# Sample columns of the gate/up projections: from chunk 0 into the combined products, in both FFNs

## The chip, the cores and the metric

The kernel runs on one core of a Trainium2 chip. The metric is the device time of one execution in microseconds; before the change three runs gave 1936.32, 1937.20 and 1937.89 us, so the median is 1937.2 us. All arithmetic is float32. The large matmuls use the type float32r on operands that are split into a high and a low part, so that each product takes three matmuls.

## The reference

One layer of a hybrid decoder trunk is computed for 1024 prompt tokens and for 64 sample tokens (8 sequences of 8), with shared weights and a model width of 1024:

```
x = x + 0.5 * rms_norm(swiglu(rms_norm(x, g1), ffn1_w_gu, ffn1_w_down), p1)
h = rms_norm(x, gm);  z = h @ w_in + b_in
    attention heads: window 128 with sinks; samples against a cache of 128 keys
    recurrent heads: gated linear recurrence in chunks of 64, state 128 x 128 per head
x = x + rms_norm(concat(norm(attention), gate(recurrence)) @ w_out, pm)
x = x + 0.5 * rms_norm(swiglu(rms_norm(x, g2), ffn2_w_gu, ffn2_w_down), p2)

swiglu(x): g, u = split(x @ w_gu);  (silu(g) * u) @ w_down      # w_gu: 1024 x 5632, w_down: 2816 x 1024
```

All rows of `x @ w_gu` are independent of each other, so a token may be computed in any group of columns.

## The kernel before, in words

**Tokens.** Three chunks: chunk 0 holds 256 prompt tokens and the 64 sample tokens (320 columns), chunks 1 and 2 hold 384 prompt tokens each (`WIDTH`, L26). Activations lie with features on partitions and tokens along the free axis.

**Gate and up of chunk 0.** For each of the 22 column tiles `j` of the gate weights and its partner of the up weights, eight row blocks are accumulated with three matmuls each (`mm3`, L260 to L262). `load_w` brings a 128x1024 weight tile into one of three raw buffers, ScalarE casts it to the high part (`wsph`, L240) and VectorE subtracts it to get the low part (`wspl`, L241). The gate then goes through silu and is multiplied with the up part (`gated0`, L712 to L728). In the first FFN the matmuls run before the norm's factor is known, so gate and up are each multiplied with the factor `rb` afterwards.

**Gate and up of chunks 1 and 2.** They are computed together, by seven products in place of eight: the token chunks and the two halves of the features make a 2x2 block matrix, and the feature halves and gate/up of the weights another (`CHAIN`, `factor`, `product`, `evict`, L751 to L815). There are 22 units `u` with 7 products of 4 row blocks. The left operands are the seven factors `SF[1..7]` (sums and differences of the activations, `sums_s`, L525 to L538), each split into high and low parts by `factor` (L466). For the first FFN the stream `p1` makes them while the chunk-0 columns run; for the second FFN the streams `c1` and `c2` do.

**Where chunk 0 runs.** In the first FFN, 18 of 22 columns run ahead of the combined products; the last four run as `piece`s between the products of the first four units, with the weight tiles that these units have split anyway. In the second FFN, the columns are used as work for TensorE beside the mixer: 4 before the end of the second chunk's mixer, 9 and then 1 before the third chunk's output projection, and 8 after it (`HEAD2`, L1681).

**What sets the order.** The program is written as streams (generators), which `tick` advances by a rate for each step of the main work; `need` runs a stream to its end. A scheduler then lays down the order of each engine. An engine works in its order, so a matmul that waits holds all behind it.

**Down projections.** Chunk 0's activations are read back from a DRAM buffer (`acts`) and multiplied with the down weights (320 columns); chunks 1 and 2 use seven products again, in pairs, from the DRAM buffers `FA`, `FB`, `FH`.

## Time and profile before

| | |
|---|---|
| median of three runs | 1937.2 us |
| span of the profiled execution, first to last instruction | 1937.4 us |
| TensorE busy | 1923.1 us (99%) |
| VectorE busy | 1430.7 us (74%) |
| ScalarE busy | 946.0 us (49%) |
| GpSimd busy | 186.1 us (10%) |
| DMA | 375.56 MB, 194 GB/s on the mean |
| mean granted TensorE clock | 0.999 |

The profile gives no time for the profiled execution beside its span; the span lies 0.2 us above the median of the runs. In the rows, PE is TensorE, PEld its weight loads, DVE VectorE, ACT ScalarE, POOL GpSimd, SP the engine that issues most transfers. The length of a matmul in a row includes its passage through the array; how fast matmuls follow each other is read from their starts. Names such as `mm<-h,wsph` stand for output and inputs.

### The profile page before, as it was taken

What the parts mean: (1) busy time and instruction counts of PE and PEld (TensorE: products, weight loads), DVE (VectorE), ACT (ScalarE), POOL (GpSimd) and SP (SyncE); (2) the same over time, 40 slices, a digit from 0 to 9 for tenths busy, and PEclk for the clock granted to TensorE, in tenths of its full rate; (3) what the DMA queues carried; (4) which work ended last, traced back from release to release, by engine and by line L of the source; (5) the groups of instructions that cost most, each with busy time, mean ns of one, the idle gap of its engine ahead of it and who ended that gap; (6) DMA issues with size and microseconds to landing.
All of it is one profiled execution on the core that took longest, in us unless ns stands there. A gap on an engine that the chain in (4) does not pass through costs nothing.

```text
span 1937.4 us, 34843 instructions
## 1 busy us (share of the span) xinstructions
PE 1923.1 (99%) x13547; PEld 1806.1 (93%) x13547; DVE 1430.7 (74%) x2469; ACT 946.0 (49%) x1701; POOL 186.1 (10%) x227
## 2 busy tenths in 40 slices
PE   9999999999999999999999999999999999999998
PEld 9999999999998987788999888989999999999886
DVE  6896789877568666787678758756987887656666
ACT  5553444444455434545445545846544444445452
POOL 0300000000004022020221212000000000000102
PEclk9999999999999999999999999999999999999999
DMA  6643676555767556765334344546555555667974
GB/s 248 209 133 115 232 267 247 206 191 184 242 217 242 180 155 215 283 220 163 114 102 153 99 140 142 164 147 209 185 198 192 198 188 189 210 228 241 308 255 141
DMA packets 175750, 375.56 MB, mean 194 GB/s; under 512 B 16144, under 2 KB 67536, under 8 KB 175568
## 3 DMA queue, kind: packets, MB, share of 16 engines
q1 hardware_dynamic: 169680, 362.84, 56.0%
q10 hardware_dynamic: 5904, 10.49, 1.5%
q8 instruction: 106, 1.74, 0.4%
q14 instruction: 60, 0.49, 0.1%
HBM read 290.86 MB, written 83.39 MB: 193 GB/s over the span
## 4 chain that ended last, share of the span: by engine, by line
PE 88%; DMA 6%; DVE 3%; ACT 1%; issue 1%; POOL 1%; SPq 0%; ACTq 0%; DVEq 0%; POOLq 0%
PE mm L260 27%; PE mm L262 26%; PE mm L261 26%; DMA ar<-fa 1%; DMA xt<-in_x_rest_dram 1%; DMA ar<-act 1%; PE lv L1337 1%; PE sc L1237 1%; DMA raw<-in_ffn_w_gu_dram 1%; PE pv L1283 1%; DVE w L241 1%; PE pT L1269 1%; PE c L262 0%; PE c L260 0%; PE c L261 0%
## 5 line engine op out<-in xcount | busy, mean ns | idle before, releaser
L260 PE MATMUL mm<-h,wsph 128*128 128x320 f32 (+1 forms) x1344 | 427.2, 319 | 0.4 <-DVE big L814 0.4
L261 PE MATMUL mm<-h,wsph 128*128 128x320 f32 (+1 forms) x1344 | 425.5, 317 | 0.2 <-DVE h L241 0.2
L262 PE MATMUL mm<-h,wspl 128*128 128x320 f32 (+1 forms) x1344 | 422.6, 316 | 0.0
L241 DVE TENSOR_TENSOR wspl<-raw,wsph 128x1024 fp32r<-128x1024 f32 x208 | 260.8, 1255 | 125.2 <-ACT wsph L240 124.1
L240 ACT CAST wsph<-raw 128x1024 fp32r<-128x1024 f32 x208 | 217.8, 1049 | 254.0 <-PE mm L261 199.3
L260 PEld LDWEIGHTS mm<-h,wsph 128*128 128x128 f32 x1344 | 252.2, 188 | 4.2 <-issue 2.3
L261 PEld LDWEIGHTS mm<-h,wsph 128*128 128x128 f32 x1344 | 252.5, 188 | 3.9 <-issue 2.3
L262 PEld LDWEIGHTS mm<-h,wspl 128*128 128x128 f32 x1344 | 251.9, 188 | 3.4 <-issue 3.1
L240 ACT CAST w<-raw 128x512 fp32r<-128x512 f32 (+1 forms) x208 | 153.8, 745 | 199.9 <-PE mm L261 96.2
L261 PE MATMUL mm<-h,w 128*128 128x384 f32 (+1 forms) x736 | 245.6, 334 | 0.3 <-DVE h L622 0.3
L260 PE MATMUL mm<-h,w 128*128 128x384 f32 (+1 forms) x736 | 245.7, 334 | 0.2 <-ACT h L620 0.2
L262 PE MATMUL mm<-h,w 128*128 128x384 f32 (+1 forms) x736 | 239.6, 333 | 0.5 <-POOL w L613 0.4
L241 DVE TENSOR_TENSOR w<-raw,w 128x512 fp32r<-128x512 f32 (+1 forms) x208 | 178.3, 861 | 72.6 <-ACT w L240 71.7
L261 PE MATMUL mm<-w,h 128*128 128x512 f32 x462 | 180.5, 391 | 0.7 <-DVE w L241 0.7
L260 PE MATMUL mm<-w,h 128*128 128x512 f32 x462 | 180.8, 394 | 0.0
L262 PE MATMUL mm<-w,h 128*128 128x512 f32 x462 | 179.8, 391 | 0.0
L260 PE MATMUL mm<-big,w 128*128 128x384 f32 x528 | 176.7, 335 | 0.3 <-ACT big L806 0.2
L261 PE MATMUL mm<-big,w 128*128 128x384 f32 x528 | 176.5, 334 | 0.0
L262 PE MATMUL mm<-big,w 128*128 128x384 f32 x528 | 176.0, 334 | 0.0
L261 PEld LDWEIGHTS mm<-h,w 128*128 128x128 f32 x736 | 138.1, 188 | 1.1 <-DVE h L622 0.8
L260 PEld LDWEIGHTS mm<-h,w 128*128 128x128 f32 x736 | 138.1, 188 | 0.8 <-ACT h L620 0.5
L262 PEld LDWEIGHTS mm<-h,w 128*128 128x128 f32 x736 | 137.6, 188 | 1.0 <-POOL w L613 0.7
(367 smaller groups left out, 3353.8 us busy)
## 6 DMA issues: line engine op xcount, KB each, us to landing
raw<-in_ffn_w_gu_dram SPq DMA_DIRECT2D x162, 512.0 KB
raw<-in_ffn_w_down_dram SPq DMA_DIRECT2D x74, 512.0 KB
raw<-in_w_in_dram SPq DMA_DIRECT2D x54, 512.0 KB
ar<-fa SPq DMA_DIRECT2D x70, 384.0 KB
big<-in_ffn_w_down_dram SPq DMA_DIRECT2D x88, 256.0 KB
fb<-big SPq DMA_DIRECT2D x44, 512.0 KB
fa<-big SPq DMA_DIRECT2D x22, 768.0 KB
raw<-fb SPq DMA_DIRECT2D x30, 512.0 KB
```

The lines of the kernel that those rows point to most:

```text
L240: made['S'] = S.copy(hi, src).ins
L241: (lo_eng or V).tensor_tensor(lo, src, hi.bitcast(F32), op=ALU.subtract)
L260: PE.matmul(out, a[0], b[0], start=first, stop=False, skip_group_check=resume)
L261: PE.matmul(out, a[0], b[1], start=False, stop=False, skip_group_check=resume)
L262: return PE.matmul(out, a[1], b[0], start=False, stop=last, skip_group_check=resume).ins
L1237: PE.matmul(banks[g][rows(hq), i, cs], zq[rows(g), 2 * pr + i, b * P + 64 * hq:b * P + 64 * hq + 64], kx[rows(g), k0 + cs.start:k0 + cs.st ...
L1269: PE.transpose(tb2[hq][:, g, i, slot], pt[g][rows(hq), c:c + P], ident[rows(hq), rows(hq)])
L1283: PE.matmul(ob[par][rows(g), :, hq], vn[rows(par), b + (blk + hq) // 2, rows(g)], pT[hq][rows(par), g, :, PLACE[hq][blk]], start=alone or ...
L1337: PE.matmul(b5[32 * i:32 * i + 32, b, a], K[:, a, cs], Q[:, a, cs], start=True, stop=True)
```

## The change

The 64 sample columns leave chunk 0 for the gate and up projections of both FFNs: chunk 0 streams `WU` = 256 columns, and chunks 1 and 2 carry 32 samples each, `WS` = 416 columns. The sample columns of the gated product are stored from the combined units into `acts` (a new small store in each unit), so the down projection stays as it is with 320 columns. In the first FFN the norm's factor is no longer multiplied to the up part; it is kept in DRAM (`rootd`) and multiplied to the chunk-0 prompt columns when the down projection leaves PSUM. In the second FFN the mixer's output stage writes the sample columns to DRAM (`extra`), and the combined operands read them from there.

All 22 columns of chunk 0 now run ahead of the combined products in both FFNs, so the `piece`s and the eighth split weight are gone. The combined products no longer wait for the whole stream of factors in the program: `product` advances the stream until its own factor is there (`feed`). One of the factors' subtractions goes to GpSimd. In the second FFN the columns are spread 3, 8 + 1 and 10 where they were 4, 9 + 1 and 8.

The wider tiles need room. The pools of small buffers shrink (`t2` 8 to 7, `small` 10 to 5, `wf` 4 to 3), and masks and constants of the mixer are made in the mixer or kept in DRAM. The norm's gain of the attention output is applied after the transpose.

```diff
+WU, XT = 256, 32
+WS = 384 + XT
...
-        return pp.tile([P, 4, w], F32R, tag=f"h{w}", bufs=8 if w == 384 else 4, name=uid("h"))
+        return pp.tile([P, 4, WS if w == 384 else w], F32R, tag=f"h{w}", bufs=8 if w == 384 else 4, name=uid("h"))
-    def big(dt=F32, shape=(P, 4, 384)):
+    def big(dt=F32, shape=(P, 4, WS)):
...
+    def feed(name):
+        gen = streams[name][0]
+        while True:
+            yield next(gen)
...
-        return pp.tile([P, 4, 8], F32, tag="small", bufs=10, name=uid("sm"))
+        return pp.tile([P, 4, 8], F32, tag="small", bufs=5, name=uid("sm"))
...
-    def tmp2(name, shape=(P, 512)):
-        return pp.tile(list(shape), F32, tag="t2", bufs=8, name=uid(name))
+    def tmp2(name, shape=(P, 512), dt=F32):
+        return pp.tile(list(shape), dt, tag="t2", bufs=7, name=uid(name))
...
     def factor(SF, m, src):
-        hi, lo = SF[m] = new(), new()
+        hi, lo = new(), new()
         S.copy(hi, src)
         yield
-        V.tensor_tensor(lo, src, hi.bitcast(F32), op=ALU.subtract)
+        (G if m in (5,) else V).tensor_tensor(lo, src, hi.bitcast(F32), op=ALU.subtract)
+        SF[m] = hi, lo
...
         def gated0(j, g, rb):
-            w = WIDTH[0]
+            w = WU
...
             def rest(u):
-                v = u
-                if rb is not None:
-                    v = tmp2("su")
-                    V.tensor_tensor(v[:, :w], u[:, :w], rb, op=ALU.mult)
-                V.tensor_tensor(t[:, :w], t[:, :w], v[:, :w], op=ALU.mult)
-                return nc.sync.dma_start(acts[:, j], t[:, :w]).ins
+                V.tensor_tensor(t[:, :w], t[:, :w], u[:, :w], op=ALU.mult)
+                return nc.sync.dma_start(acts[:, j, :w], t[:, :w]).ins
...
         def product(u, m):
+            while m not in f.SF:
+                next(f.feed)
             c, first, last = CHAIN[m]
             if first:
                 chains[u, c] = mmbank()
-            bk = chains[u, c][:, :384]
+            bk = chains[u, c][:, :WS]
...
             elif m == 3:
                 V.tensor_tensor(e[:, 1], bk, e[:, 1], op=ALU.add)
                 act(0)
+                nc.sync.dma_start(acts[:, j, WU:].rearrange("p (h t) -> p h t", h=2), e[:, 0:3:2, 384:])
...
                         if kp == NK - 1:
-                            S.copy(y[hf][:, i, :w], bank[:, :w])
+                            if tag == 1:
+                                V.tensor_tensor(y[hf][:, i, :WU], bank[:, :WU], rt, op=ALU.mult)
+                                S.copy(y[hf][:, i, WU:w], bank[:, WU:w])
+                            else:
+                                S.copy(y[hf][:, i, :w], bank[:, :w])
...
-            V.scalar_tensor_tensor(o[:r], o[:r], sm[:r, 1, 0:1], aon[:r], op0=ALU.mult, op1=ALU.mult)
+            S.activation(o[:r], o[:r], AF.Copy, scale=sm[:r, 1, 0:1])
...
-    RA0, RA1, RB0, RB1 = 1.2, 0.75, 0.6, 0.8
-    HEAD1, HEAD2 = 9, (4, 13, 22)
+    RA0, RA1, RB0, RB1, RB2 = 1.2, 0.75, 0.6, 0.8, 1.1
+    HEAD1, HEAD2 = NK, (3, 11, 22)
...
+        xs.append(load_x(1))
         for j in first[3:]:
+            if j == first[3]:
+                stream("p1", p1(), P1)
             stored = f1.up0(j, w0)
-            if j in XAT:
+            if j == first[3]:
                 with tc.issue_after(stored):
-                    xs.append(load_x(len(xs)))
...
-        f1.begin(units(HEAD1))
-        need("p1")
+        f1.begin(UNITS)
+        f1.feed = feed("p1")
...
-        f2.begin(units(NK))
-        need("c2")
+        f2.begin(UNITS)
+        f2.feed = feed("c2")
```

How the order moves, at three places.

TensorE, where the first FFN goes from chunk 0 to the combined products. `mm` with 320 columns is chunk 0, `c` a piece of it beside the units; before:

```order
L262 MATMUL mm_1450<-h_143,wspl_1377 128x320
L260 MATMUL mm_1513<-h_142,wsph_1413 128x320
L261 MATMUL mm_1513<-h_144,wsph_1413 128x320
L260 MATMUL c_266_1658<-h_142,w_1576 128x320
L261 MATMUL c_266_1658<-h_144,w_1576 128x320
L262 MATMUL mm_1513<-h_142,wspl_1414 128x320
```

and now:

```order
L245 MATMUL mm_1740<-h_136,wsph_1682 128x256
L246 MATMUL mm_1740<-h_134,wspl_1683 128x256
L244 MATMUL mm_1821<-h_723,w_1800 128x416
L245 MATMUL mm_1821<-h_724,w_1800 128x416
L246 MATMUL mm_1821<-h_723,w_1800 128x416
```

The pieces are gone: 256-column matmuls stand up to the last, and then only 416-column products.

VectorE, in the first FFN's chunk-0 columns, where the sums and factors are made (`wspl`: the low part of a weight tile; `sg`: gate and product; the wide `big`: sums, and `L460` a factor's low part). Now:

```order
L225 TENSOR_TENSOR wspl_1233<-raw_1230,wsph_1232 128x1024
L521 TENSOR_TENSOR big_1170<-big_1169,big_409 128x1664
L523 TENSOR_TENSOR big_494<-big_409,big_494 128x1664
L225 TENSOR_TENSOR wspl_1272<-raw_1269,wsph_1271 128x1024
L186 TENSOR_TENSOR lbe<-cols,lbe 128x4
L187 TENSOR_TENSOR lbe<-cols,lbe 128x4
L710 TENSOR_TENSOR sg_1303<-mm_1267,rb_307 128x256
L714 TENSOR_TENSOR sg_1227<-sg_1227,mm_1191 128x256
L225 TENSOR_TENSOR wspl_1309<-raw_1306,wsph_1308 128x1024
L525 TENSOR_TENSOR big_410<-big_410,big_1170 128x1664
L460 TENSOR_TENSOR h_1301<-big_495,h_1300 128x1664
L460 TENSOR_TENSOR big_1186<-big_1170,big_1185 128x1664
```

The wide rows were 1536 elements long and are 1664 now, and a column has two rows of 256 where it had three of 320.

TensorE, at the last attention block of the third chunk, in the second FFN's chunk-0 columns (`sc`: scores, `pT`: transposes of the probabilities, `pv`: their product with the values). Before, the end of the 33 matmuls between `sc` and `pT`:

```order
L262 MATMUL mm_14023<-h_11489,wspl_13883 128x320
L260 MATMUL mm_14023<-h_11489,wsph_13882 128x320
L261 MATMUL mm_14023<-h_11491,wsph_13882 128x320
L262 MATMUL mm_14023<-h_11489,wspl_13883 128x320
L260 MATMUL mm_14023<-h_11489,wsph_13882 128x320
L1269 MATMUL pT_13953<-ident,t_2011_13924 128x64
```

and now all that stands there:

```order
L1254 MATMUL sc_13911<-kx_10609,big_10724 64x192
L246 MATMUL mm_14051<-hh_11548,wspl_14061 128x256
L244 MATMUL mm_14051<-hh_11548,wsph_14060 128x256
L245 MATMUL mm_14051<-hh_11548,wsph_14060 128x256
L246 MATMUL mm_14051<-hh_11548,wspl_14061 128x256
L1286 MATMUL pT_13949<-ident,t_2000_13920 128x64
```

Four chunk-0 matmuls are left between the scores and the transposes, and after them `pv` follows with no chunk-0 matmul between.

295 lines of the change are left out of this document (156 added, 139 removed).

## The prediction, as put on record

> **What bounds the kernel now.** I read the page's first part, then the share of busy time by stage, then the matmul groups with their shapes kept apart, then single matmuls in order of time. The page's busy row comes first:
>
> ```profile
> PE 1923.1 (99%) x13547; PEld 1806.1 (93%) x13547; DVE 1430.7 (74%) x2469; ACT 946.0 (49%) x1701; POOL 186.1 (10%) x227
> PE 88%; DMA 6%; DVE 3%; ACT 1%; issue 1%; POOL 1%; SPq 0%; ACTq 0%; DVEq 0%; POOLq 0%
> ```
>
> TensorE is busy 99% of the span and carries 88% of the chain that ended last (second row). Busy is not the same as at its peak, so I look at three stages: the first FFN's chunk-0 columns, its combined products, and the second FFN's combined products (columns: stretch, its length, busy us and instructions of PE, PEld, DVE, ACT, POOL, clock, DMA share, GB/s).
>
> ```profile
> 100.00:150.00 50.00, 50.00 (x336) 50.00 (x335) 48.28 (x66) 25.91 (x35) 0.00 (x0) 1.00 0.46 146
> 310.00:360.00 50.00, 50.00 (x290) 50.00 (x289) 44.23 (x79) 23.37 (x46) 0.00 (x0) 1.00 0.65 235
> 1390.00:1500.00 110.00, 110.00 (x636) 110.00 (x636) 92.63 (x160) 48.97 (x96) 0.00 (x0) 1.00 0.56 195
> ```
>
> In order of time (start us, length us), runs of matmuls of 320, of 384 and of 512 columns, first and last of each:
>
> ```profile
> 22.97 0.30 PE L260 MATMUL ax<-h,w 128*128 128x320 f32 x1
> ...
> 29.86 0.31 PE L262 MATMUL ax<-h,w 128*128 128x320 f32 x1
> ...
> 349.83 0.33 PE L262 MATMUL mm<-big,w 128*128 128x384 f32 x1
> ...
> 351.91 0.33 PE L262 MATMUL mm<-h,w 128*128 128x384 f32 x1
> ...
> 1799.81 0.39 PE L260 MATMUL mm<-w,h 128*128 128x512 f32 x1
> ...
> 1803.66 0.39 PE L262 MATMUL mm<-w,h 128*128 128x512 f32 x1
> ```
>
> The ends lie 47, 12 and 17 matmuls apart. That is a start every 0.1466 us at 320 columns, 0.1733 at 384 and 0.2265 at 512. The three lie on one line: 0.41667 ns for each column and 13.3 ns for each matmul (0.1467, 0.1733, 0.2267). 290 matmuls in 50 us and 636 in 110 us are that step and nothing else. So the stages that this change touches most are bound by the number of columns that TensorE streams, and not by a wait.
>
> **What the change removes and adds on TensorE.** It leaves the number of matmuls alone and moves columns. Chunk 0 has 22 column tiles of the gate and 22 of the up weights, 8 row blocks each, 3 matmuls each: 1056 in an FFN, 2112 in both. They go from 320 to 256 columns. The combined products are 22 units x 7 products x 4 blocks x 3 = 1848 in an FFN, 3696 in both (the groups below: 3 x (704 + 528)). They go from 384 to 416.
>
> ```profile
> L260 PE MATMUL mm<-h,w 128*128 128x384 f32 x704 | 235.4, 334 | 0.0
> L260 PE MATMUL mm<-big,w 128*128 128x384 f32 x528 | 176.7, 335 | 0.3 <-ACT big L806 0.2
> L260 PE MATMUL c<-h,w 128*128 128x320 f32 x64 | 19.7, 308 | 0.0
> ```
>
> *Chunk 0.* No float32r matmul of 256 columns is in the trace. The line gives 0.1200 us, so 2112 x 0.0267 = 56.3 us less. The nearest rows bound it: 320 columns from above (0.1467, no gain), and from below the narrowest pairs of a 128-column weight load and a matmul that stand back to back:
>
> ```profile
> 1004.18 1.03 PEld L1461 LDWEIGHTS u<-big,t 128*128 128x128 f32 x8
> ```
> ```profile
> 1004.35 1.05 PE L1461 MATMUL u<-big,t 128*128 128x128 f32 x8
> 1005.24 0.49 PE L1138 MATMUL vT<-ident,t 128*128 128x128 f32 x3
> ```
>
> Eight pairs take 1005.24 - 1004.35 = 0.89 us, 0.111 each (gain at most 2112 x 0.0356 = 75 us). I take the line, since 0.120 lies above the fastest pair seen.
>
> *Combined products.* 416 lies between two measured widths; the line gives 0.1867, so 3696 x 0.0133 = 49.3 us more. If the step stayed at 0.1733 it would be nothing, and at the 512 step 3696 x 0.0534 = 197 us; three points on a line leave little room for either.
>
> TensorE's own account is therefore -56.3 + 49.3 = **-7.0 us**, a small difference of two large terms. Of these, the addition is sure, because the combined stages have no slack. The gain is only real if weights still arrive in time at the faster pace.
>
> The Trainium skill, page "TensorE: Matmul & The Clock Gate", section "Back-to-back issue gap", gives a sustained pace of loads and matmuls of about 81 ns at 128 columns and 131 ns at 512, which is 0.13 ns a column; by it the account would be -17.6 + 15.4 = -2.2 us. This trace does not agree: 0.2267 us at 512 columns, and 0.42 ns a column.
>
> **Whether the narrower stage is fed.** A column tile is 24 matmuls: 3.52 us now, 24 x 0.120 = 2.88 us then. Preparing it costs one load, one cast and one subtraction; the other rows of this stage (window 36 to 165 us) are the products with the factor and the first factors of the combined products:
>
> ```profile
> L241 DVE TENSOR_TENSOR wspl<-raw,wsph 128x1024 fp32r<-128x1024 f32 x26 | 35.0, 1346 | 6.1 <-ACT wsph L240 6.1
> L725 DVE TENSOR_TENSOR su<-mm,rb 128x320 f32<-128x320 f32 x15 | 7.3, 484 | 0.4 <-PE mm L262 0.4
> L471 DVE TENSOR_TENSOR h<-big,h 128x1536 fp32r<-128x1536 f32 x4 | 7.0, 1748 | 0.0
> ```
> ```profile
> L240 ACT CAST wsph<-raw 128x1024 fp32r<-128x1024 f32 x25 | 26.2, 1047 | 26.1 <-PE mm L261 18.2 <-DMA raw<-in_ffn_w_gu_dram 6.1 <-issue 1.1
> ```
>
> ACT mostly waits for TensorE (18.2 of 26.1 us): it runs as far ahead as four pairs of weight tiles allow. The lead is then three tiles less cast and subtraction; at 2.88 us, 8.6 - 1.05 - 1.22 = 6.4 us. What eats it is the end of the factors (sums and first factors) on VectorE. Here is what it eats today, the subtraction of two tiles and TensorE's first matmul with each:
>
> ```profile
> 100.44 1.22 DVE L241 TENSOR_TENSOR wspl<-raw,wsph 128x1024 fp32r<-128x1024 f32 x1
> 122.33 1.22 DVE L241 TENSOR_TENSOR wspl<-raw,wsph 128x1024 fp32r<-128x1024 f32 x1
> ```
> ```profile
> 109.04 0.31 PE L260 MATMUL mm<-h,wsph 128*128 128x320 f32 x1
> ...
> 126.64 0.31 PE L260 MATMUL mm<-h,wsph 128*128 128x320 f32 x1
> ```
>
> The lead falls from 7.4 us (109.04 - 101.66) to 3.1 (126.64 - 123.55) over five tiles, and TensorE does not stall. In the changed order the same stretch has, over six tiles, 8 wide operations (1.67 us from start to start, times 416/384: 1.81), 6 subtractions (1.14) and 7 products of 256 columns (0.34), with 0.5 for small ones: 24.2 us of VectorE for 6 x 2.88 = 17.3 us of TensorE. That eats 6.9 of the 6.4 us: a stall of **+0.5 us**. Ends: 0 if the lead is fuller, 6.9 if there is none. The fifth factor's subtraction, which goes to GpSimd, lengthens neither. The second FFN has more of this work before its last ten columns, so I count nothing there. The product `su` and its copy are dropped: VectorE had cover for them, so they gain nothing.
>
> **Where cover goes in the mixer.** The second FFN's chunk-0 columns also fill TensorE while attention runs. Between the second chunk's last block and the third output projection, 9 columns now stand for 10, and narrower ones: 51.8 us for 70.4. The order shows where it runs out: at the last attention block, 33 matmuls of 0.147 us stood between its scores and the transposes of its probabilities; now 4 of 0.120. The chain that they covered (a score group, the last maximum, the last exponential, the transposes, their copy, the product with the values):
>
> ```profile
> 1265.51 0.83 PE L1237 MATMUL sc<-kx,big 64*64 64x192 f32 x16
> 1266.27 0.41 PE L261 MATMUL mm<-h,wsph 128*128 128x320 f32 x1
> ...
> 1272.22 0.59 PE L1269 MATMUL pT<-ident,t 64*128 64x64 f32 x12
> ...
> 1273.66 0.89 PE L1283 MATMUL pv<-t,vn 64*64 64x128 f32 x24 [0.36 <-DVE t L1274]
> ```
> ```profile
> 1269.59 0.19 ACT L1255 ACTIVATION_READ_ACCUMULATOR t<-t,sm 128x1 f32 x1
> ```
>
> Scores are issued by 1266.27 and the exponentials end at 1269.78: 3.5 us, of which 0.5 is covered now, so 3.0 open. From the transposes' end to the product is 0.85 us (1272.81 to 1273.66), with nothing between in the new order, there and at the block before. Together 4.7, less the 0.36 that is lost there already: 4.3. I take **+3.5**, because at the block before, the transposes stand in two pieces with others between, so their first copy can start early. Ends: 0 (the softmax ends before TensorE gets there) and 4.3.
>
> **Counted at nothing:** the factor's product at the first down projection (on VectorE instead of ScalarE, behind 18 matmuls of the other banks, 18 x 0.147 = 2.6 us; without that cover 0.4 us each for four banks); the strided stores of the left factors and the reload of masks (DMA share 0.46 to 0.65 above); the mixer's constants, moved behind the down products. SP's queue gains 44 small stores of sample columns, each waiting for a product on VectorE with the next raw loads behind it. It waits for VectorE in the combined stage already, without TensorE feeling it (window 310 to 460 us: us, times, longest):
>
> ```profile
> SPq L826 <- DVE big L825: 17.1, 5, 3.5
> ```
>
> If a raw load came late by such a wait in each unit, 22 x 3.5 = 77 us would be the price in one FFN; the loads of a unit are issued a unit (15.7 us) ahead, so I see no path for it.
>
> Sum against the profiled execution's 1937.4: -7.0 + 0.5 + 3.5 = -3.0, 1934.4. The runs' median is 0.2 lower, so **1934.2 us**, 0.16% faster. A change under 0.2% (3.9 us) can't be told from none here, so this sits at the edge of what shows.
>
> **Rivals.**
> *The waits vanish* (the exponentials end early, the lead holds): the full -7.0, 1930.2. For it: a column fewer leaves 2 x (1.05 + 1.22) us less of casts and subtractions beside that chain on ScalarE and VectorE. Against: the adjacent rows in the order.
> *The raw buffers set the pace* (slower). A tile's buffer is used again after three tiles: 8.64 us. A load takes
>
> ```profile
> 299.83 4.31 DMA raw<-in_ffn_w_gu_dram
> ```
>
> plus issue 0.33, cast 1.05 and subtraction 1.22: 6.9 us, so 1.7 us of waiting are free. VectorE is busy 48.28 of 50 us there, so waits of 2 to 3 us are likely at times. If the mean turn is 9.5 us, a tile takes 3.17, and over the 58 tiles that have no mixer beside them 58 x 0.29 = 17 us are lost: about 1951.
> *The weight load sets the pace* (slower). The loads above stand (1.03 - 0.19) / 7 = 0.120 us apart. If the matmul's 13.3 ns come on top, a step is 0.133 and the gain 2112 x 0.0137 = 29 us: 1962. Against: the matmuls of those same loads started 0.111 apart. The same page, section "LDWEIGHTS (loading the stationary operand)", gives 107 ns for 128 columns, under the 0.111 seen, and so speaks against this rival.
> *Fewer small buffers* (`t2` 7 for 8, `small` 5 for 10) make attention and recurrence wait for each other in the mixer, some 6 us: 1940.
>
> **How the numbers follow.** Forecast 0.58 (1930.5 to 1938), waits vanish 0.13, raw buffers 0.13, weight load 0.05, small buffers 0.11. Faster by over 0.2% (below 1933.3): 0.13 and 0.27 of the forecast, 0.40. Slower by over 0.2% (above 1941.1): 0.13 + 0.05 + 0.06 of the small buffers, 0.24. Within: 0.36. The range for 8 in 10 is 1929 to 1943; the slow rivals beyond it hold 0.18.
>
> **What would show it.** Right: starts 0.120 us apart at 256 columns and 0.187 at 416; under 2 us of TensorE idle before the first combined product; a gap of about 3 us between the last block's scores and transposes. Wrong: a step at 256 columns other than 0.120 (0.002 us there is already 4.2 us), ACT waiting for the raw loads and TensorE for `wspl` in the chunk-0 stages, or waits of attention for `sm`.

## The result: slower by 2.2%, and the profile after

The changed kernel takes 1981.04 us (median of 4 runs, 1977.39 to 1983.25) against 1937.55 us before (4 runs, 1936.32 to 1939.19): 1.0219 times as long, 95% interval 1.0204 to 1.0234. The forecast was 1934.2, the range 1929 to 1943. The profiled execution spans 1975.7 us, 38.3 more than before; it is the fastest of the four (1977.39 us, mean granted clock 0.997), and the others took 1980.6 to 1983.3 us at 0.992 to 0.994, so what follows accounts for 38 us and not for the 43.5 between the medians.

The page's first part and its chain, after:

```profile
PE 1945.5 (98%) x13547; PEld 1807.3 (91%) x13547; DVE 1454.2 (74%) x2474; ACT 963.1 (49%) x1719; POOL 202.2 (10%) x230
PE 78%; DMA 8%; DVE 7%; ACT 3%; issue 2%; POOL 1%; SPq 0%; ACTq 0%; DVEq 0%; POOLq 0%
```

TensorE's share of the chain falls from 88% to 78%: waits for VectorE and for transfers have come into it. The same three stretches as in the prediction (stretch, length, busy us and instructions of PE, PEld, DVE, ACT, POOL, clock, DMA share, GB/s):

```profile
100.00:150.00 50.00, 46.57 (x367) 45.57 (x367) 41.17 (x49) 24.78 (x32) 4.73 (x1) 1.00 0.53 175
310.00:360.00 50.00, 50.00 (x266) 49.52 (x265) 43.22 (x74) 22.27 (x42) 0.00 (x0) 1.00 0.59 209
1390.00:1500.00 110.00, 109.02 (x576) 107.43 (x576) 88.06 (x147) 46.22 (x87) 0.00 (x0) 1.00 0.53 183
```

In the chunk-0 stretch TensorE now stands still for 3.4 of 50 us. In the combined stretches it is busy as before (109.02 of 110 us in the second), with fewer instructions. Runs of matmuls of 256, 416 and 512 columns in order of time (start us, length us), first and last of each:

```profile
64.49 0.28 PE L245 MATMUL mm<-h,wsph 128*128 128x256 f32 x1
...
67.13 0.28 PE L246 MATMUL mm<-h,wspl 128*128 128x256 f32 x1
...
349.47 0.35 PE L246 MATMUL mm<-big,w 128*128 128x416 f32 x1
...
351.92 0.35 PE L246 MATMUL mm<-h,w 128*128 128x416 f32 x1
...
1899.23 0.39 PE L244 MATMUL mm<-w,h 128*128 128x512 f32 x1
...
1903.19 0.40 PE L246 MATMUL mm<-w,h 128*128 128x512 f32 x1
```

They lie 22, 13 and 17 matmuls apart: a start every 0.1200, 0.1885 and 0.2329 us. The line of the prediction (0.41667 ns a column and 13.3 ns) gives 0.1200, 0.1867 and 0.2267. The narrow step is exact; 416 columns are 2 ns too long, and the 512-column products, whose width the change does not touch, are 6 ns longer than before. Over all neighbouring matmuls of one width the means are 0.1735 (384) and 0.2274 (512) before, 0.1890 (416) and 0.2332 (512) after.

I cut both traces at the same matmuls, and set each stretch against what its float32r matmuls take on the line (us, before and after):

| from, to | length | change | of it on the line | rest |
|---|---|---|---|---|
| start, first combined product | 136.6, 144.7 | +8.1 | -0.6 | +8.7 |
| first FFN, combined products | 353.5, 355.6 | +2.1 | -2.8 | +4.9 |
| to the mixer's first scores | 231.3, 231.5 | +0.2 | 0.0 | +0.2 |
| to the last block's transposes | 549.6, 539.2 | -10.4 | -22.1 | +11.7 |
| to the second FFN's first combined product | 101.9, 106.2 | +4.3 | -6.1 | +10.4 |
| second FFN, combined products | 325.0, 354.6 | +29.6 | +24.5 | +5.1 |
| to the last matmul | 230.8, 235.4 | +4.6 | +0.2 | +4.4 |

The line sums to -6.9, as forecast (-7.0). What was missed is 45 us in the last column. Some 18 us are the longer steps: 8 at 416 columns and 10 at 512, worked out in the section on the prediction; they are most of the three rows that hold hardly a wait (both combined stages and the last stretch). Of the other 27 us, 16 are idle time of TensorE (span less busy time: 14.3 before, 30.2 after), and up to 5 are two stretches at half clock that follow waits (an estimate: half their length; last section). The rest is not attributed. The longest waits of TensorE in the first head (up to 146 us) and from the mixer to the second FFN (733 to 1379 us), after (us in total, times, longest):

```profile
PE rb L279 <- POOL ss L295: 2.6, 1, 2.6
PE mm L244 <- DVE sg L710: 2.6, 2, 1.4
...
PE mm L244 <- DVE sg L714: 1.0, 1, 1.0
...
PE mm L246 <- DVE wspl L225: 2.7, 2, 2.3
PE pv L1300 <- DVE t L1291: 2.7, 2, 1.8
PE pT L1286 <- ACT t L1272: 1.7, 2, 1.5
PE mm L244 <- ACT sg L1059: 1.5, 2, 0.9
PE mm L244 <- ACT h L1223: 1.1, 1, 1.1
```

Of these only the pair of `pT` and `pv` was foreseen. Is it VectorE's time that holds TensorE in the heads, or do the weights arrive late? ScalarE does wait longer for raw loads: in the first head 26.0 us (9.2 before). But around TensorE's later waits in the first head, and around the long one for `wspl` in the second, VectorE has hardly an idle moment (columns as above; VectorE is the third busy time):

```profile
92.00:118.00 26.00, 22.71 (x184) 21.96 (x183) 26.00 (x25) 15.68 (x15) 6.85 (x1) 1.00 0.41 139
1342.00:1364.00 22.00, 18.62 (x149) 17.81 (x148) 21.89 (x15) 13.27 (x13) 4.84 (x1) 1.00 0.30 107
```

So there it is VectorE's queue that is late, and not a load.

### The profile page after: what moved, and what is told of

The parts are those of the page before. It is cut to its first block, busy times and chain, and to the rows that moved or that the text cites. A ratio compares the mean times of both kernels' runs of the same rounds, so it can differ in the third digit from the quotient of the medians.

```text
span 1975.7 us, 35138 instructions
## 1 busy us (share of the span) xinstructions
PE 1945.5 (98%) x13547; PEld 1807.3 (91%) x13547; DVE 1454.2 (74%) x2474; ACT 963.1 (49%) x1719; POOL 202.2 (10%) x230
## 4 chain that ended last, share of the span: by engine, by line
PE 78%; DMA 8%; DVE 7%; ACT 3%; issue 2%; POOL 1%; SPq 0%; ACTq 0%; DVEq 0%; POOLq 0%
PE mm L244 24%; PE mm L246 24%; PE mm L245 24%; DMA raw<-in_ffn_w_gu_dram 4%; DVE wspl L225 2%; ACT wsph L224 1%; DMA big<-in_ffn_w_down_dram 1%; PE lv L1354 1%; DMA ar<-fa 1%; DMA ar<-act 1%; PE pv L1300 1%; DVE w L225 1%; DVE t L748 1%; PE sc L1254 0%; PE pT L1286 0%
## 5 line engine op out<-in xcount | busy, mean ns | idle before, releaser
L225 DVE TENSOR_TENSOR wspl<-raw,wsph 128x1024 fp32r<-128x1024 f32 x216 | 268.9, 1247 | 120.6 <-ACT wsph L224 113.2
L224 ACT CAST wsph<-raw 128x1024 fp32r<-128x1024 f32 x216 | 226.1, 1048 | 250.5 <-PE mm L245 157.2
L244 PE MATMUL mm<-h,wsph 128*128 128x320 f32 (+2 forms) x1056 | 328.4, 313 | 3.9 <-DVE sg L710 2.6
L245 PE MATMUL mm<-h,wsph 128*128 128x320 f32 (+2 forms) x1056 | 328.6, 311 | 0.1
L246 PE MATMUL mm<-h,wspl 128*128 128x320 f32 (+2 forms) x1056 | 326.8, 310 | 0.8 <-DVE wspl L225 0.6
L246 PE MATMUL mm<-h,w 128*128 128x416 f32 (+1 forms) x736 | 257.1, 350 | 0.7 <-POOL w L607 0.5
L244 PE MATMUL mm<-h,w 128*128 128x416 f32 (+1 forms) x736 | 256.4, 348 | 0.2
L245 PE MATMUL mm<-h,w 128*128 128x416 f32 (+1 forms) x736 | 255.0, 346 | 0.6 <-DVE h L616 0.3
L244 PEld LDWEIGHTS mm<-h,wsph 128*128 128x128 f32 x1056 | 198.8, 189 | 8.6 <-issue 4.1
L245 PEld LDWEIGHTS mm<-h,wsph 128*128 128x128 f32 x1056 | 199.6, 189 | 4.1 <-issue 3.3
L246 PEld LDWEIGHTS mm<-h,wspl 128*128 128x128 f32 x1056 | 199.4, 189 | 2.9 <-DVE wspl L225 1.5
L246 PE MATMUL mm<-big,w 128*128 128x416 f32 x528 | 186.3, 353 | 1.3 <-DVE w L225 1.3
L244 PE MATMUL mm<-big,w 128*128 128x416 f32 x528 | 185.6, 351 | 0.4 <-ACT big L796 0.4
L245 PE MATMUL mm<-big,w 128*128 128x416 f32 x528 | 184.7, 350 | 0.0
L224 ACT CAST w<-t 128x512 fp32r<-128x512 f32 x176 | 108.1, 619 | 94.1 <-PE mm L246 91.3
L245 PEld LDWEIGHTS mm<-h,w 128*128 128x128 f32 x736 | 138.4, 188 | 3.2 <-DVE h L616 1.2
L244 PEld LDWEIGHTS mm<-h,w 128*128 128x128 f32 x736 | 138.2, 188 | 1.9 <-ACT big L798 0.4
```

Source lines behind the costliest of these rows:

```text
L224: made['S'] = S.copy(hi, src).ins
L225: (lo_eng or V).tensor_tensor(lo, src, hi.bitcast(F32), op=ALU.subtract)
L244: PE.matmul(out, a[0], b[0], start=first, stop=False, skip_group_check=resume)
L245: PE.matmul(out, a[0], b[1], start=False, stop=False, skip_group_check=resume)
L246: return PE.matmul(out, a[1], b[0], start=False, stop=last, skip_group_check=resume).ins
```

## The experiments

Three theories were to be told apart from rivals: that the long steps come from where operands lie in SBUF; that chunk-0 tiles had been cover for other engines, so that making them shorter is worth less than the line says; and that the new waits come from single edits (a subtraction on GpSimd, fewer buffers, the mixer's new code). Times are medians, each beside runs of the kernel before on the same chip (1936.9 to 1938.4 in every comparison).

**The first term alone.** The kernel before, in which chunk-0 matmuls stream 256 columns:

```diff
-                mm3(bank[:, :w], ..., hcol(h[0], k, w), first, last)
+                n = 320 if first else 256      # first of a bank only
+                PE.matmul(out[:, :n], a[0], b[0][:, :n], start=first, ...)
+                PE.matmul(out[:, :256], a[0], b[1][:, :256], ...)
+                PE.matmul(out[:, :256], a[1], b[0][:, :256], ...)
```

> The kernel before with 256 instead of 320 columns in 2024 of its 2112 chunk-0 matmuls (the first of each bank keeps 320; the sample columns of both FFNs' hidden layers are left out, so the outputs differ); nothing else is changed, VectorE and ScalarE still work on 320 columns. This is the prediction's first term alone. If TensorE sets the pace wherever a chunk-0 tile stands: 2024 x 26.7 ns = 54 us, 1882 to 1886. Theory 'tiles as cover': where VectorE or the mixer's chains set the pace, a shorter tile only lengthens the waits. First head: 22 us shorter on TensorE, but VectorE is busy 103 of 117 us there, so some 10 to 13 us come; mixer: 14 of the tiles, 18 us, of which about half comes; second head 10 us, half of it; the four tiles inside the first FFN 5 us, all of it: -28 to -38 us, 1900 to 1909.

Measured: 1911.81 us, 0.9864 (0.9849 to 0.9879): 26.6 us gained of 54. The window from 60 us to the first combined product, before (to 137.8) and in this kernel (to 126), then its waits for VectorE in the head and ScalarE in the second FFN, and in the mixer:

```profile
60.00:137.80 77.80, 77.80 (x531) 77.53 (x530) 72.67 (x93) 42.12 (x54) 8.98 (x6) 1.00 0.51 161
```
```profile
60.00:126.00 66.00, 60.36 (x469) 59.75 (x468) 63.17 (x81) 39.20 (x50) 11.01 (x6) 0.95 0.54 174
```
```profile
PE mm L266 <- DVE su L731: 5.6, 2, 3.3
PE mm L260 <- ACT w L240: 3.6, 2, 3.1
PE pv L1290 <- DVE t L1281: 3.1, 2, 2.3
PE pT L1276 <- ACT t L1262: 1.7, 2, 1.5
```

VectorE was busy 93% of this window before (72.67 of 77.80) and is busy 96% now (63.17 of 66.00); TensorE waits for it, and its mean clock is 0.95 there. In the kernel before, from the mixer on, `pT` had no such wait and `pv` a short one:

```profile
PE pv L1283 <- DVE t L1274: 0.5, 2, 0.4
```

Change by stretch, in us (on the line, then measured): first head -22.3, -11.8; the four tiles inside the first FFN -4.6, -5.5; from the mixer's first scores to the end of the second FFN's combined products -27.0, -11.8. So half of the prediction's first term does not exist, without any other edit. Two things qualify this. VectorE and ScalarE still work on 320 columns here and make the product `su`, which the change drops, so VectorE may hold TensorE longer in this first head than in the changed kernel's. And part of the loss is the clock: four stretches at half clock, 20.5 us in all, follow the waits, which costs up to 10 us (an estimate: half their length). The theory of cover stands; what it forecast was still too high by 1 to 11 us, 3.1 of them a wait for weights at the second FFN's combined products.

**Where operands lie.** First, every buffer moved by 32 bytes, in the changed kernel and in the one before:

```diff
-    cp = ctx.enter_context(tc.tile_pool(name="cp", bufs=1))
+    cp = ctx.enter_context(tc.tile_pool(name="cp", bufs=1)); cp.tile([P, 8], F32, name="pad")
```

> The changed kernel with one unused constant of 32 bytes per partition put ahead of all others: every buffer in SBUF starts 32 bytes further on, so that the matmuls' operands start 32 bytes past a multiple of 64 (as they do in the kernel before) instead of on one; nothing else differs. Theory 'addresses': the steps that came out longer than the line (0.2333 us at 512 columns instead of 0.2267, 0.1890 at 416 instead of 0.1867) do so because of where the operands start; they go back to 0.2267 and 0.1867, which gives 1870 x 6.5 ns = 12 us and 3697 x 2.3 ns = 8.5 us, so that the span falls by about 20 us, to 1953 to 1960. Rival 'width': the step of 416 columns is what it is, and 512 columns are slower because of the stationary tiles' pitch of 1664 bytes: steps and span stay (1975 to 1982).

> The kernel before with the same unused 32 bytes ahead of all others: its buffers now start on a multiple of 64 bytes, as the changed kernel's do; nothing else differs. Theory 'addresses': the step at 512 columns goes from 0.2267 to 0.2333 us (1860 matmuls, +12 us), the one at 384 columns from 0.1733 to about 0.176 (4500 matmuls, +6 to +13 us), the one at 320 columns by little; span 1952 to 1963. Rival 'width': no step moves, 1935 to 1940.

Measured: 1982.3 and 1937.63 us (1.0000, 0.9991 to 1.0009); the 512-column step stays at 0.2332 in the one and at 0.2273 in the other. The theory of common addresses fell. Pairing the steps of the trace after with the addresses in the program suggested something else: steps are on the line when the moving operand and the neighbouring stationary operands start at the same place modulo 256 bytes. Before, all do, by these addresses. In the changed kernel rows of 416 columns are 1664 bytes apart, 6.5 times 256, so every second row starts 128 bytes off. The test puts just that into the kernel before:

```diff
+        pp.tile([P, 32], F32, tag="pad1", ...)   # ahead of the split weights
+        pp.tile([P, 32], F32, tag="pad2", ...)   # behind the raw buffers
```

> The kernel before with an unused 128 bytes ahead of the split-weight buffers and another 128 bytes behind the raw buffers: the split weights now start 128 bytes off from all other matmul operands, taken modulo 256 bytes, where before all operands start at the same place modulo 256; the instructions are the same. Theory 'phase' (a matmul is longer when its moving operand and its neighbours' stationary operands start at different places modulo 256 bytes, as the rows of 1664 bytes make them do in the changed kernel): the 1865 matmuls of 512 columns go from 0.2267 to about 0.233 us (+12 us), the 2400 of 384 columns that read split weights from 0.1735 to about 0.176 (+6 us), those of 320 columns hardly move; span 1948 to 1957. Rival 'row length' (rows of 1664 bytes, not the starts, make it): no step moves, span 1934 to 1939.

Measured: 1951.51 us, 1.0075 (1.0060 to 1.0090): 13.7 us lost by 256 bytes of padding, with the same instructions. Its 512-column matmuls, 17 apart:

```profile
1849.82 0.39 PE L264 MATMUL mm<-w,h 128*128 128x512 f32 x1
...
1853.78 0.40 PE L265 MATMUL mm<-w,h 128*128 128x512 f32 x1
```

That is 0.2329 us a step; at 384 columns the mean goes from 0.1735 to 0.1748 for the combined products, at 320 nothing to speak of shows. The rival 'row length' is out, since no row length changed. Now the way back, in the changed kernel, for all that is not a combined factor:

```diff
-        return [[hslot(n), hslot(n)], [hslot(n), hslot(n)]]
+        return [[flat(n), flat(n)], [flat(n), flat(n)]]     # rows 4 * w bytes apart, same buffer
-                t = hslot(1).rearrange(...)[:, :, :, :384]
+                t = flat(1).rearrange(...)
-        f1.pool = tp
+        f1.pool = tp; tp.tile([P, 32], F32, name="pad")     # f2.pool too
```

> The changed kernel with the rows of the 384-column tiles that are no combined factors (the mixer's input and output, the pair products' activations) laid 1536 bytes apart instead of 1664, in the same buffers, and the FFN pools moved by 128 bytes, so that in the 512-column products all operands start at the same place modulo 256 bytes again; the combined factors keep rows of 1664 bytes. Theory 'phase': the 512-column step goes back from 0.2333 to about 0.227 us, 1865 x 6 ns = 11 us, the 416-column step stays at 0.189, and the median falls from 1981 to 1968 to 1972. Rival 'row length' gives the same here; rival 'a slower TensorE clock or contention in the later stages': no change, 1978 to 1984.

Measured: 1972.04 us (1969.55 to 1975.03), 9.0 less than the changed kernel. The 512-column step, 18 matmuls apart, is back:

```profile
1849.74 0.39 PE L248 MATMUL mm<-w,h 128*128 128x512 f32 x1
...
1853.82 0.39 PE L248 MATMUL mm<-w,h 128*128 128x512 f32 x1
```

(4.08 / 18 = 0.2267), and the last stretch takes 231.0 us instead of 235.4. Last, the 416-column rows:

```diff
-                mm3(bk, ..., (hi[:, k], lo[:, k]), ...)
+                o = slice(k * WS - k % 2 * XT, (k + 1) * WS - k % 2 * XT)
+                mm3(bk, ..., (hi[:, o], lo[:, o]), ...)     # rows flattened
```

> The kernel of after_flat (512-column operands in phase again, median 1972.0) whose combined products read the odd rows of a factor 32 columns early, so that the 416 columns of every row start at the same place modulo 256 bytes as the weights; the columns read are the wrong ones, so the outputs differ, the work is the same. Theory 'phase': the 416-column step falls from 0.189 to 0.1867 us, 3696 x 2.2 ns = 8 us: 1962 to 1966. Rival 'row length' (1664 bytes between rows, wherever they start): the step stays at 0.189 and the median at 1970 to 1975.

Measured: 1967.35 us (1962.28 to 1970.21), 4.7 less than after_flat, though the ranges just overlap, and between what theory and rival gave; the mean step falls from 0.1888 to 0.1879, not to 0.1867. So phase explains all of the 512-column loss, and a little under half of the 416-column one (0.9 of 2.1 ns); steps of 183 to 185 and of 189 to 191 ns alternate there even with all operands in phase, and what makes that is open.

**The first head.** GpSimd's sums left out:

```diff
-            sum_squares(G if add else V, ss[:, :w], sq[:, :w], d)
+            if d == 1 or not add: sum_squares(V, ss[:, :w], sq[:, :w], d)
```

> The changed kernel without the sums of squares that GpSimd adds up for the first FFN's chunks 1 and 2 (12 additions of 416 columns, 21 us of GpSimd, left out; the mean root is taken of two of the eight parts only, so the outputs differ). The first head takes 144.7 us up to the first combined product, 12.8 us of them above the line. Theory 'shared port': while GpSimd adds, VectorE's operations are stretched (a weight's low half 2.11 us instead of 1.22), and it is VectorE's lateness that holds TensorE: without the additions the head loses 5 to 9 us of the 12.8. Rival 'one wait': only the mean root's matmul waits for GpSimd, 2.6 us, and the later waits for gates (1.5, 1.4 and 0.7 us at 103 to 113 us) stay: 2 to 3 us gained. Rival 'weights late': raw loads set the pace, under 1 us gained.

Measured in a single execution (1975.29 us): the head takes 144.2 us (144.7 in the changed kernel), half a microsecond less. But this execution has two stretches of 3.4 us at half clock in the head, at 13.3 and 112.3 us, and the changed kernel's trace has none there. They cost up to 3.4 us (an estimate: half their length), so at the same clock the gain would lie between 0.5 and 3.9 us: less than the theory of the shared port asks (5 to 9), and in keeping with the 2 to 3 us of the rival 'one wait'. Part of what is gained goes again, since another wait grows (for `wspl`, 2.8 us). One run can't tell more. Another GpSimd operation costs more visibly. VectorE and GpSimd around factor 5's low half, in both heads of the changed kernel:

```profile
98.05 1.89 DVE L523 TENSOR_TENSOR big<-big,big 128x1664 f32<-128x1664 f32 x1
99.85 1.23 DVE L225 TENSOR_TENSOR wspl<-raw,wsph 128x1024 fp32r<-128x1024 f32 x1
100.98 3.76 DVE L186 TENSOR_TENSOR lbe<-cols,lbe 128x4 f32<-128x4 f32 x1
...
1345.22 1.89 DVE L521 TENSOR_TENSOR big<-big,big 128x1664 f32<-128x1664 f32 x1
1347.02 5.50 DVE L523 TENSOR_TENSOR big<-big,big 128x1664 f32<-128x1664 f32 x1
```
```profile
97.88 6.85 POOL L460 TENSOR_TENSOR h<-big,h 128x1664 fp32r<-128x1664 f32 x1 [23.75 <-ACT h L458]
...
1345.92 4.84 POOL L460 TENSOR_TENSOR h<-big,h 128x1664 fp32r<-128x1664 f32 x1 [82.14 <-ACT h L458]
```

A subtraction of 4 columns takes 3.76 us and ends with GpSimd's (104.74 and 104.73). The Trainium skill, page "SBUF — State Buffer", section "Who interferes with whom", names a pair of ports that VectorE and GpSimd lock against each other for a whole instruction. The rows agree: in the second head GpSimd's operation starts during one of VectorE's (which ends at 1347.11) and ends 3.65 us after it, at 1350.76; VectorE's next one ends 1.76 us later still, at 1352.52, where one alone takes 1.88. The lengths in these rows include the time held. The edit undone:

```diff
-        (G if m in (5,) else V).tensor_tensor(lo, src, ...)
+        V.tensor_tensor(lo, src, ...)
```

> The changed kernel with the low half of factor 5 of both FFNs subtracted by VectorE again instead of GpSimd. In the trace after, while GpSimd makes it (6.8 us in the first FFN, 4.8 in the second), one VectorE operation is held until it ends: 3.76 us instead of 0.16 for a 128x4 subtraction, 5.50 instead of 1.88 for a 128x1664 one. Theory 'held port': 3.6 us of VectorE come back at each head and 1.9 are added; the waits of TensorE for gates and low halves behind them (1.5, 1.4 and 0.7 us in the first head, 0.5, 0.7 and 2.5 in the second) shrink by half or more: -3 to -6 us in all (1975 to 1978). Rival 'VectorE is overbooked anyway': the added 1.9 us eat the gain, within 1 us of the change (1980 to 1982).

Measured: 1976.22 us (1974.63 to 1979.91), 4.8 less by the medians. The ranges overlap (the changed kernel's begins at 1977.39), but the trace shows where the gain lies: first head 142.2 us (144.7), last mixer transposes to the first combined product 103.2 (106.2), and the 4-column subtraction takes 0.15 again. The first head takes 144.3 to 147.5 us in the seven traces in which its instructions are those of the changed kernel, so 142.2 is outside their spread. And the feeding spread out:

```diff
-    RA0, RA1, RB0, RB1, RB2 = 1.2, 0.75, 0.6, 0.8, 1.1
+    RA0, RA1, RB0, RB1, RB2 = 1.2, 0.75, 0.6, 0.8, 0.75
-P1 = 1.0
+P1 = 0.7
```

> The changed kernel with the feeding of the combined factors spread over the whole of each head: 0.7 steps per tick instead of 1.0 in the first (50 steps over 72 of its 76 ticks instead of the first 50), 0.75 instead of 1.1 in the second (27 steps over 36 of 40 ticks instead of 25). Theory 'crowding': VectorE is late because the feeding's operations come too close together; spread, the heads lose 4 to 8 us less than the 9 and 7 us they lose now (1973 to 1977). Rival 'too little VectorE time in all': what is spread is late at the first combined products instead, 1979 to 1985.

Measured: 1976.93 us (1974.96 to 1977.90), 4.1 less: the heads give 2.8 and 3.9 us, and the first FFN's combined products take 2.4 back, with a new wait of 2.2 us. That wait is not for a factor: ScalarE copies a product's bank late, after 2.5 us of waiting for a raw load. (In the second FFN they take 1.2 us more, about what they vary from trace to trace.) So the work is crowded, as the theory says; that there is too much of it in all, as the rival says, this run doesn't show.

**The mixer's last blocks.** The tiles laid out as before the change:

```diff
-    HEAD1, HEAD2 = NK, (3, 11, 22)
+    HEAD1, HEAD2 = NK, (4, 13, 22)
```

> The changed kernel with the second FFN's 22 chunk-0 tiles laid out 4, 9, 1, 8 as in the kernel before, instead of 3, 8, 1, 10: two more of them stand among the last mixer blocks, two fewer ahead of the second FFN's first combined product. Theory 'cover': the waits of the last attention blocks (transposes pT 4.1 us more than before, scores sc 1.9, pv 1.7, oT 1.4) come from too little tile work between them, and two more tiles take about half of these 9 us away; ahead of the first combined product the feeding of the factors loses up to 5.8 us of cover, so the net lies between -5 and +2 us (1972 to 1980). Rival 'latency of the mixer alone': the waits move with the blocks and stay as long, and the lost cover shows in full: 1978 to 1987.

Measured: 1978.26 us (1974.58 to 1980.82), 2.8 less, within the spread of the runs. The waits `pv` 2.7 and `pT` 1.7, of which the theory expected half to go, are the same: the transposes and products of these blocks still follow each other with nothing between. So the rate was moved, by what the order showed:

```diff
-    RM = [0.88, 1.08, 1.24]
+    RM = [0.88, 1.08, 1.20]
```

> The changed kernel with one number changed: the third mixer's steps come at 1.20 per tick instead of 1.24. By the order of the instructions on TensorE, the changed kernel puts no tile work between the transposes pT and the products pv of the third-last attention block, 0.5 us between the last block's scores and its transposes, and none between those and its products (before: 4.0, 4.8 and 0.3 us); at 1.20 there stand 3.9, 6.3 and 4.5 us. Theory 'cover': the waits of these blocks (1.8, 0.5, 0.9, 1.5, 0.9 and 1.2 us in the trace after) go, and with them the two stretches of half clock behind them (3.3 and 1.7 us): -7 to -12 us, 1969 to 1974. Rival 'the mixer's own edits or its fewer buffers': the waits reappear at other blocks, 1977 to 1982.

Measured: 1988.09 us (1986.83 to 1992.40), 7 more than the changed kernel. My theory fell in this form: the waits left those places and came back, longer, elsewhere. TensorE's waits from the mixer to the second FFN, in this kernel:

```profile
PE mm L244 <- ACT sg L1059: 7.0, 4, 3.3
PE oT L1219 <- ACT t L1213: 4.7, 1, 4.7
PE mm L246 <- DVE wspl L225: 2.3, 1, 2.3
PE kT L1463 <- DVE h L1224: 1.5, 1, 1.5
PE pv L1300 <- DVE t L1291: 1.3, 1, 1.3
```

Why it takes 7 us more is not shown. One price of a tile among the blocks stands in this trace, on ScalarE: ahead of a tile's gate it loads a table for 1.28 us, in the middle of the mixer's chain (start us, length us; the longest wait for `sg` ends with these two rows):

```profile
1226.88 1.28 ACT L1059 ACT_TABLE_LOAD   x1
1228.17 0.38 ACT L1059 ACTIVATE sg<-mm 128x256 f32<-128x256 f32 x1
```

Between the first scores and the second FFN's first combined product there are 21 such loads here, 19 in the changed kernel and before; so a tile's place in the order also decides how often ScalarE loads. How much of the 7 us that is, no run shows. Are the mixer's own edits to blame for its waits? The end of each block as before (a copy and a subtraction, the scale on VectorE):

```diff
-            S.activation(o[:r], o[:r], AF.Copy, scale=sm[:r, 1, 0:1])
+            V.tensor_scalar(o[:r], o[:r], sm[:r, 1, 0:1], None, op0=ALU.mult)
-            for c in range(4): ...   # four scaled copies, four subtractions
+            put_mix(n, 0, sl, b4[:, :, :r])
```

> The changed kernel with the end of each attention block as before: the scale by the root on VectorE, one copy and one subtraction for the halves instead of four scaled copies and four subtractions (the gains of the output norm are left out, so the outputs differ). Theory 'tiles as cover': the waits in the last blocks come from the shorter tiles between them, and change by no more than 1.5 us a block at the two or three blocks that wait: -1 to -4 us, 1977 to 1980. Rival 'the mixer's own edits': these chains are what makes the last blocks late: -7 us and more, below 1974.

Measured: 1980.54 us (1978.31 to 1983.12), no change; so this edit is not the cause. And the buffers, in the kernel before:

```diff
-  tag="small", bufs=10      tag="t2", bufs=8      tag="wf", bufs=4
+  tag="small", bufs=5       tag="t2", bufs=7      tag="wf", bufs=3
```

> The kernel before with the changed kernel's numbers of buffers: 5 small tiles instead of 10, 7 two-kilobyte tiles instead of 8, 3 weight buffers in the FFN pools instead of 4 (all operands kept in phase). The prediction's rival 'fewer buffers' gives 1940 and more; theory 'buffers cost nothing': 1936 to 1939.

Measured: 1939.41 us, 1.0014 (1.0004 to 1.0023): 2.5 us, just outside what I had for "nothing" and a tenth of the 27 us of waits. With before_256, where the kernel before gets about the same `pv` and `pT` waits (3.1 and 1.7 us; 2.7 and 1.7 after) from shorter tiles alone, this leaves cover as the cause of these two. The other edits of the mixer (masks and constants made in it, the store of the sample columns) have no run of their own.

**All together.**

> The changed kernel with four edits together: the 384-column rows 1536 bytes apart (after_flat, -9.0 us by its median), factor 5's low half on VectorE (after_v5, -4.8), the feeding spread over the heads (after_rates, -4.1), the third mixer at 1.20 steps per tick (after_rm, expected -7 to -12). If each acts at its own place they add up, but for the two that act on the heads, which share some 3 us: -22 to -28, 1953 to 1959. If they overlap more, 1960 to 1966. Neither is below the kernel before (1937.5): what stays is the 416-column step (8 us), the rest of the heads' waits, against a gain of 7 us on the line.

> The changed kernel with after_flat and after_v5 (-9.0 and -4.8 us by their medians), the first head's feeding at 0.8 steps per tick, and more cover in the mixer: the second FFN's chunk-0 tiles laid out 4, 11, 1, 6 instead of 3, 8, 1, 10, with the third mixer at 1.07 steps per tick, so that its 64 steps use all of 60 ticks. Theory 'tiles as cover': the mixer's and the second head's waits shrink by 5 to 9 us: 1957 to 1963. Rival 'the feeding needs the tiles more': the six tiles left before the second FFN's first combined product do not cover the feeding of its factors, and the 5 to 9 us are lost there: 1966 to 1973.

Measured: 1968.18 us (1967.27 to 1970.58) and 1962.88 us (1961.51 to 1963.87). The first misses both of its ranges; it holds after_rm's edit, which had lost 7 us where 7 to 12 were expected to be gained. The second, with four more columns beside the mixer than the changed kernel (16 for 12) and four fewer behind it, is the best version of the change, some 18 us under it and 1.0129 times (1.0112 to 1.0145) the kernel before. From the first scores to the second FFN's first combined product, with the same columns in between, it takes 14.2 us less than the changed kernel (after_v5 alone: 2.6); that stage's combined products take 5.8 back, with one wait:

```profile
PE mm L248 <- ACT w L228: 6.8, 1, 6.8
```

Around that wait (1350 to 1372 us) VectorE is busy for 21.89 of 22 us, mostly with factors. So both its theory and the rival show: cover that the mixer gets is missing for the feeding. That a slower mixer with more tiles gained here and after_rm lost is the one open point of this part.

## Why the prediction was wrong, point by point

*What bounds the kernel.* Right for the combined stages, wrong as a rule: "busy 99%" was read as bound by TensorE. With steps on the line a stage is at TensorE's pace, but that says nothing of how far the next engine is behind. VectorE's 48.28 of 50 us stood in the quoted rows.

*Chunk 0, -56.3 us: the step that failed.* "I take the line": the step at 256 columns is 0.1200, as forecast, to the digit. But the term multiplied its gain by all 2112 matmuls, as if TensorE set the pace beside every one of them. Alone the term is worth 26.6 us of 54 (before_256), since the tiles stand beside the feeding in the two heads and beside the mixer, and there part of a tile's time was needed by VectorE and by the mixer's chains. "The gain is only real if weights still arrive in time" named a condition of this kind; the sum then charged 4 us for it (+0.5 and +3.5), where before_256 shows some 27 and the same rows of the table after the change 31 (8.7, 11.7 and 10.4, with 3 to 4 of longer steps in them).

*Combined products, +49.3 us.* Mis-sized: 3696 x (0.1890 - 0.1735) = 57 us. The line was drawn through widths whose rows keep the operands in phase; at 416 columns they don't, which is a little under half of the 8 us, and the rest is open. *Not in the sum at all:* the 512-column products, 1865 x about 0.0055 = 10 us, whose buffers changed their row length with `WS`. The first term as measured, these two, -28.4 (the span's change in before_256) + 57 + 10, give 39 us where 38.3 were measured; so close a sum is partly luck, since factor 5, the feeding, the tiles' layout and the stretches at half clock differ too.

*The first head, +0.5 (0 to 6.9).* Measured 8.7 beyond the line, outside the bound. The right engine was named, but the balance of the lead counted VectorE's operations at their undisturbed lengths, over six tiles only, and left out the wait for the root of GpSimd's sums (2.6 us). "The fifth factor's subtraction, which goes to GpSimd, lengthens neither" is false: it holds VectorE for 3.6 us in each FFN. For the second FFN "I count nothing there" is false too: TensorE waits 2.3 us for one low half.

*The mixer, +3.5 (0 to 4.3).* The right mechanism at the right block (`pT` waits 1.5 us, `pv` 0.9), but it was sought only at the last block. An earlier block (its products start at 1218 us) has no work between its transposes and its products either (1.8 us, and 0.5 and 0.9 behind it); the prediction counted such a block, and then let it off because its transposes stand in two pieces.

*Counted at nothing.* Down product, small stores, masks and constants: the stretch from the first FFN's down products to the first scores is unchanged (+0.2), so no loss shows there. What a wait does to the clock was not counted (below).

*Rivals.* The weight load as pace (1962) comes nearest in number, by luck: the step of 0.1200 excludes it. Raw buffers (1951) are on the right side, and their sign came, ScalarE waiting for raw loads (26.0 us in the first head for 9.2); but where TensorE waits, it is for gates and low halves that VectorE makes late, with 26.00 of 26 us busy. No run had a fourth raw buffer, so what the loads add stays open. Small buffers: 2.5 us, not 6. The forecast's 0.58 rested on a small difference of two large terms, only one of which was certain.

## What to carry to other kernels

Before work is taken from the busiest engine, ask for each stage which engine comes next and how far behind it is: a matmul column is worth its time only where no other engine needs that time for its own work, while a column added to a stage without slack is paid in full. When a row's length in SBUF changes, look at all matmuls that read these buffers, also those whose shape stays the same. Measure one term alone when the forecast is the difference of two large ones.

## What the runs showed of the hardware that was not expected

**Phase of operands.** A float32r matmul of 512 columns takes 0.2267 us from start to start when the moving operand and the stationary operands around it start at the same place modulo 256 bytes, and 0.2329 when they are 128 apart (the only distance that was tried); 384 columns 0.1735 and 0.1748 (combined products). At 320 columns nothing to speak of showed, and no run put 256 columns to the test. Moving all together by 32 bytes does nothing. The Trainium skill, page "SBUF — State Buffer", section "Who interferes with whom", has TensorE read its two operands by two independent ports; in these runs the pace depends on how the two operands lie to each other; why is open.

**A wait costs twice.** The trace after, at a stall of 1.82 us (start us, length us; then stretches with PE, PEld, DVE, ACT, POOL, clock, DMA share, GB/s):

```profile
1218.11 0.69 PE L1300 MATMUL pv<-t,vn 64*64 64x128 f32 x12 [1.82 <-DVE t L1291]
...
1222.92 0.41 PE L245 MATMUL mm<-hh,wsph 128*128 128x256 f32 x1
1223.13 0.41 PE L246 MATMUL mm<-hh,wspl 128*128 128x256 f32 x1
```
```profile
1215.83:1219.24 3.41, 1.16 (x25) 0.78 (x23) 3.01 (x4) 3.41 (x10) 0.29 (x2) 1.00 0.70 257
1218.00:1219.00 1.00, 0.69 (x12) 0.45 (x12) 1.00 (x3) 1.00 (x4) 0.00 (x0) 1.00 0.51 154
1219.40:1226.00 6.60, 5.71 (x44) 5.01 (x45) 4.49 (x24) 5.00 (x10) 0.00 (x0) 0.50 0.67 222
1226.00:1227.00 1.00, 1.00 (x10) 1.00 (x10) 0.17 (x1) 1.00 (x1) 0.00 (x0) 0.96 0.00 0
```

The granted clock is 0.50 from 1219.4 to 1226.0 us, and 256-column matmuls start 0.21 us apart instead of 0.12. TensorE is busy for 5.71 us of it, so some 2.9 us (an estimate: half of that) are lost on top of the wait. A second such stretch, 3.4 us long, follows the last block's waits at 1271; before the change there is none ahead of the last microseconds. The Trainium skill, page "TensorE: Matmul & The Clock Gate", section "What's actually happening", has the clock fall to half after an idle window of about 3.4 us; here waits of 1.8 and 0.5 us with small transposes and 64-row products between them were enough, and TensorE was busy for 1.16 of the 3.41 us ahead of the first stretch (first row of the second fence) and 1.57 ahead of the second.

Which waits are followed by half clock differs from one trace to the next. Ahead of their last microseconds, the traces of all these runs have half clock only in stretches of 3.4, 6.8 or 10.2 us. In the changed kernel they lie at 1219 and 1274 us; in after_pad, the same program moved by 32 bytes, at 74, 115, 1276 and 1365 us. So a difference of 2 or 3 us between the same stretch of two traces should not be put down to an edit before the clock in both has been read.
